# ConvFFN up and gate products as 2x2 blocks with seven products, on one Trainium2 core

## The chip, the cores and the metric

The kernel runs on one core of a Trainium2 chip. The metric is the device time of one execution in microseconds (us), the median of several runs. The engines of a core are named as the profile names them: PE is TensorE's matmuls and PEld its weight loads, DVE the vector engine, ACT the scalar engine, POOL GpSimd, SP the engine that issues the DMAs. Each of them works through its own queue in order.

## What is computed

A two-layer trunk: each layer is a mixer (layer 0 an mLSTM and a retention mixer, layer 1 an HGRN2 mixer) and then a ConvFFN. 592 tokens pass together (16 meta tokens, 8 samples of 8, a prompt of 512), the model width is 1024 and the ConvFFN's 2816. The change touches the ConvFFN:

```python
def rms_norm(x, gain):
    y = x * lax.rsqrt(jnp.mean(x * x, axis=-1, keepdims=True) + EPS)
    return y * gain

def conv_ffn(xn, w_in, conv_w, conv_b, w_out, buf):
    u, gate = jnp.split(xn @ w_in, 2, axis=-1)
    padded = jnp.concatenate([buf, u], axis=1)
    conv = conv_b + sum(padded[:, j:j + t] * conv_w[j] for j in range(3))
    h = jax.nn.silu(conv) * gate
    return h @ w_out, padded[:, t:]
```

The result is added to the residual x. All inputs and outputs are float32.

## The kernel before

Features lie on partitions, tokens on columns. A float32 product is made of three matmuls of a 22-bit type (fp32r): every operand is split into a high part (an ACT copy) and a low part (a DVE subtraction), and high x high, high x low and low x high are added in PSUM. The residual's split parts are the moving operand; a weight tile of 128 x 128 is the stationary one.

The dense work is a list of blocks. Each block is a pair of a loader, which issues the weights' DMA and their split, and a body, which issues the products and what follows them. `stream` (L280) takes the blocks in order and keeps two weight tiles loaded ahead; `weights` (L296) loads into one of two raw buffers (L303), splits on ACT (L308) and on DVE (L310) into one of three pairs of buffers. The split is issued where the block is fetched, that is, before the body of the block in front. `interleave` (L133) mixes the mixers' own instructions between the blocks; once issued, each engine keeps the order.

`dense` (L316) makes 128 output features of all tokens: for each of eight 128-row chunks k three matmuls on each of two halves of the tokens, all through L123: 48 matmuls, of 296 columns in layer 0 and of 290 and 288 in layer 1. A `hooks` entry runs something after chunk k's matmuls are issued. PSUM has two double tiles ("mm") for such products and four single ones ("px").

`ffn` (L463) makes the ConvFFN of a layer. Its 22 `in_block`s (L474) take one 128-feature chunk each: the up product (48 matmuls), then `up` (L507 to L527), which multiplies it by 1/rms of each token (`rb`, from `norm_rows` and `norm_bcast`, hooked into block 0) on DVE and sets the convolution's edges with small POOL copies (L517 to L526); then the gate product (48 matmuls), its multiplication by 1/rms (L491), the convolution as one ACT operation (L493) and two DVE ones (L495), SiLU on ACT (L497), the gating (L501, L502), and the split of the result (L505 on ACT, L506 on DVE) into one of eight slots. 7, 7 and 8 chunks make a group. `out_proj` (L410) multiplies a group with the output weights, one block for each of eight output chunks (the first two side by side), and adds to the residual on DVE (L424); in the last group it also makes the next norm's square sums (L223, L230) and the next split parts of the residual (L215, L216). In layer 1 the last group goes over the tokens in two spans of 320 and 256 columns ("dq" in the profile, single "px" tiles). `token_proj` (L349) makes token-major products with two half weights; layer 0 begins with two of these blocks.

Of the kernel before, what the change touches and what calls it, by code (L numbers as in the profile page):

```python
# [9 lines left out]
F32 = mybir.dt.float32  # L10
# [30 lines left out]
def shape_constants():  # L41
# [44 lines left out]
    # which of a 32-row block's keys the queries of the second halves take, level by level; and the diagonal  # L86
# [13 lines left out]
def trunk_kernel(ctx: ExitStack, tc: tile.TileContext, I, O):  # L100
# [32 lines left out]
    def interleave(dense, streams, active):  # L133
        """runs `streams` in order, up to `active` at once, and `dense` whenever all of them wait"""
# [26 lines left out]
    # ------------------------------------------------------------ helpers  # L161
# [29 lines left out]
    # ------------------------------------------------------------ constants and inputs  # L191
# [40 lines left out]
    def quick_root(y, x, n):  # L232
        """1 / sqrt(x): fewer steps, with a table that the scalar engine has to load"""
# [5 lines left out]
    def norm_rows(ts=range(5), root=rsqrt):  # L239
        """1 / rms, token-major"""  # L240
# [16 lines left out]
    def norm_bcast(groups=((0, 1, 2), (3, 4))):  # L257
        """1 / rms of each token on all partitions"""
# [18 lines left out]
    # ------------------------------------------------------------ dense products  # L277
    # A block is (load, body): load() emits the weights' DMA and their split, body(w) is a generator.
    def stream(blocks):
# [11 lines left out]
        while ahead:  # L291
            w, body = ahead.pop(0)
            fetch()
            yield from body(w)

    def weights(*views):  # L296
        """views: DRAM [128, k, n]; hi/lo f32r tiles of the same shape"""
        out = []
        for v in views:
            k = v[0].shape[1]  # L300
            n = sum(a.shape[2] for a in v)
            raw = wp.tile([128, k, n], F32, name="wr", tag="wr", bufs=2)
            o = 0  # L303
            for a in v:
                ld.dma_start(out=raw[:, :, o:o + a.shape[2]], in_=a)
                o += a.shape[2]
            hi = wp.tile([128, k, n], F32R, name="wh", tag="wh", bufs=3)
            S.copy(hi, raw)  # L308
            lo = wp.tile([128, k, n], F32R, name="wl", tag="wl", bufs=3)
            V.tensor_tensor(out=lo, in0=raw, in1=hi.bitcast(F32), op=ALU.subtract)  # L310
            out.append((hi, lo))
        return out
# [30 lines left out]
    def proj(w, c0, post, first=0, hooks=None):  # L343
        """feature-major projection of the tokens from `first`"""
        def body(ww):
            (p,), off = yield from dense(ww, acts_x(), first, hooks)
# [3 lines left out]
    def token_proj(w, pieces, emit, first=False, hook=None):  # L350
        """token-major projection onto the columns of `pieces`"""
# [12 lines left out]
        def body(halves):  # L364
            p = None
            if first:
                # as the chunks of the residual come in; the norm is ready when the products are
# [30 lines left out]
    def split(src, j, scale=None):  # L398
        """src (f32 [128, NT]) * scale -> slot pair j as hi/lo."""
# [10 lines left out]
    def out_proj(w, row0, acts, c0, gain, last, ready=None, spans=(None,)):  # L410
        """blocks that add acts() @ w[row0:] to the residual chunk by chunk.  The first chunks go side by side, so
        that the last of acts() has time to come."""
        def block(ocs, span):
# [4 lines left out]
            def body(ww):  # L418
# [3 lines left out]
                ps, off = yield from dense(ww, acts(), c0, span=span)  # L422
# [11 lines left out]
    def mix_proj(w, mixed, c0, gain, src):  # L434
        """the residual comes back, and the heads' outputs go into it, half of them at a time"""
# [25 lines left out]
    # ------------------------------------------------------------ ConvFFN  # L461
    def ffn(l, next_gain, spans=(None,)):
# [10 lines left out]

        def in_block(fc):  # L474
            def body(ww):
# [4 lines left out]
                cvo, stv = env["cvo"], env["st"]  # L480
                (pu,), off = yield from dense(ww[0:1], acts_x(), c0, hooks[0])
                if fc > 0:
                    ub, b0 = up(pu, off)
                (pg,), off = yield from dense(ww[1:2], acts_x(), c0, hooks[1])
                if fc == 0:
                    ub, b0 = up(pu, off)
                rb = state["rb"]
# [964 lines left out]
```

## Time and profile before

| | us |
|---|---|
| median of 3 runs | 1631.42 |
| lowest and highest run | 1631.22 and 1632.81 |
| span of the profiled execution | 1633.1 |
| TensorE busy in it | 1584.1 |
| DVE busy in it | 938.8 |
| ACT busy in it | 625.8 |
| POOL busy in it | 204.2 |

The profiler gives no time outside its span, so the profiled execution's own time is the 1633.1 us. Layer 0's ConvFFN begins near 378 us and layer 1's near 1196 us; the last products end near 1619 us. Busy times of TensorE are modelled from the starts of its instructions, so what a matmul costs is read from the distance of one start to the next.

### The profile page before, as it was taken

The numbers are of one execution on the slowest core, as the hardware profiler recorded it, in microseconds if no ns is written. First come the engines' busy times: TensorE is split into PE (matmuls) and PEld (weight loads), VectorE is DVE, ScalarE is ACT, GpSimd is POOL, SyncE is SP. The second block draws the span as 40 slices with busy tenths as digits, with TensorE's granted clock in tenths as the row PEclk, the third lists the DMA queues.
The fourth block names the chain that finished last, engine by engine and source line by source line (L and its number), as shares of the span: only waits on it lengthen the run. The fifth ranks groups of instructions, "written<-read, shape, count | busy, mean of one in ns | idle before, by whom it ended". The sixth has DMA issues, their size and how long they took to land. (4 is left out here: it accounts for less than half of the span.)

```text
span 1633.1 us, 32234 instructions
## 1 busy us (share of the span) xinstructions
PE 1584.1 (97%) x13508; PEld 1538.7 (94%) x13508; DVE 938.8 (57%) x1933; ACT 625.8 (38%) x1114; POOL 204.2 (13%) x402
## 2 busy tenths in 40 slices
PE   4999999999999999999999899999999999999997
PEld 4999999999999999999999798898999999999997
DVE  5576564757553454355546876766675535534565
ACT  3543434334331232233345466564443213322343
POOL 4000000000110110010002525333001101100102
PEclk9999999999999999999999999999999999999998
DMA  4334435433323222322422132223233232223244
GB/s 144 97 94 100 94 89 83 141 95 95 88 73 87 78 81 75 91 78 85 146 74 66 56 102 91 61 95 96 92 101 89 71 93 84 74 85 88 80 120 135
DMA packets 236049, 149.61 MB, mean 92 GB/s; under 512 B 7512, under 2 KB 227416, under 8 KB 235904
## 3 DMA queue, kind: packets, MB, share of 16 engines
q1 hardware_dynamic: 235904, 147.56, 31.9%
q8 instruction: 106, 1.74, 0.4%
q14 instruction: 39, 0.32, 0.1%
HBM read 132.89 MB, written 14.65 MB: 90 GB/s over the span
## 5 line engine op out<-in xcount | busy, mean ns | idle before, releaser
L123 PE MATMUL dp<-h,wh 128*128 128x296 f32 (+2 forms) x2176 | 477.8, 301 | 0.8 <-ACT v_c L661 0.5
L308 ACT CAST wh<-wr 128x1024 fp32r<-128x1024 f32 (+3 forms) x240 | 234.1, 978 | 625.2 <-PE dp L123 485.5
L123 PE MATMUL dp<-xl,wh 128*128 128x296 f32 (+2 forms) x2176 | 472.1, 298 | 0.0
L123 PE MATMUL dp<-h,wl 128*128 128x296 f32 (+2 forms) x2176 | 471.7, 298 | 0.0
L123 PEld LDWEIGHTS dp<-h,wh 128*128 128x128 f32 x2176 | 351.2, 189 | 4.3 <-issue 1.8
L123 PEld LDWEIGHTS dp<-h,wl 128*128 128x128 f32 x2176 | 352.1, 189 | 0.0
L123 PEld LDWEIGHTS dp<-xl,wh 128*128 128x128 f32 x2176 | 351.8, 189 | 0.0
L310 DVE TENSOR_TENSOR wl<-wr,wh 128x1024 fp32r<-128x1024 f32 (+3 forms) x240 | 273.8, 1141 | 76.3 <-ACT wh L308 73.0
L123 PE MATMUL dp<-bh,wh 128*128 128x296 f32 (+2 forms) x832 | 182.8, 300 | 2.0 <-DVE x L424 0.5
L123 PE MATMUL dp<-bh,wl 128*128 128x296 f32 (+2 forms) x832 | 179.7, 297 | 0.0
L123 PE MATMUL dp<-bl,wh 128*128 128x296 f32 (+2 forms) x832 | 179.5, 297 | 0.0
L424 DVE TENSOR_TENSOR x<-x,dp 128x592 f32<-128x592 f32 (+2 forms) x72 | 54.9, 763 | 153.1 <-PE dp L123 153.0
L123 PEld LDWEIGHTS dp<-bh,wh 128*128 128x128 f32 x832 | 134.0, 188 | 5.9 <-ACT wh L308 2.4
L491 DVE TENSOR_TENSOR gt<-dp,rb 128x592 f32<-128x592 f32 (+1 forms) x44 | 33.7, 767 | 179.9 <-PE dp L123 179.8
L123 PEld LDWEIGHTS dp<-bl,wh 128*128 128x128 f32 x832 | 134.4, 188 | 0.0
L123 PEld LDWEIGHTS dp<-bh,wl 128*128 128x128 f32 x832 | 134.2, 188 | 0.0
L123 PE MATMUL tp<-wh,h 128*128 128x256 f32 (+3 forms) x280 | 84.6, 303 | 19.0 <-ACT wh L308 11.8
L123 PE MATMUL tp<-wl,h 128*128 128x256 f32 (+3 forms) x280 | 81.2, 290 | 0.3 <-DVE wl L310 0.3
L123 PE MATMUL tp<-wh,xl 128*128 128x256 f32 (+3 forms) x280 | 79.7, 289 | 1.9 <-DVE xl L216 1.9
L495 DVE SCALAR_TENSOR_TENSOR cv<-ub,vec,cv 128x612 f32<-128x612 f32 (+1 forms) x88 | 74.1, 842 | 1.6
L123 PEld LDWEIGHTS tp<-wh,h 128*128 128x128 f32 (+1 forms) x280 | 52.3, 187 | 24.0 <-ACT wh L308 11.8
L497 ACT ACTIVATE cv<-cv 128x612 f32<-128x612 f32 (+1 forms) x44 | 31.1, 708 | 90.8 <-DVE cv L495 90.8
(425 smaller groups left out, 1933.8 us busy)
## 6 DMA issues: line engine op xcount, KB each, us to landing
wr<-in_w_ffn_in SPq DMA_DIRECT2D x88, 512.0 KB, 3.8
wr<-in_w_in_ab SPq DMA_DIRECT2D x32, 512.0 KB, 7.0
wr<-in_w_in_c SPq DMA_DIRECT2D x32, 512.0 KB, 4.1
wr<-in_w_ffn_out SPq DMA_DIRECT2D x32, 448.0 KB, 3.5
wr<-in_w_ffn_out SPq DMA_DIRECT2D x24, 512.0 KB, 3.8
x<-in_x SPq DMA_DIRECT2D x16, 296.0 KB, 5.1
out_H<-s_s SPq DMA_DIRECT2D x8, 576.0 KB, 2.9
wr<-in_w_out_ab SPq DMA_DIRECT2D x16, 256.0 KB, 2.9
```

The source lines that it names most:

```text
L123: T.matmul(out, lhsT=lhsT, rhs=rhs, **kw)
L308: S.copy(hi, raw)
L310: V.tensor_tensor(out=lo, in0=raw, in1=hi.bitcast(F32), op=ALU.subtract)
L424: V.tensor_tensor(out=x[oc][:, a:b], in0=x[oc][:, a:b], in1=p[:, off + a:off + b], op=ALU.add)
L491: V.tensor_tensor(out=gt[:, h0:], in0=pg[:, off + h0:off + NT], in1=rb[:, h0:], op=ALU.mult)
L495: V.scalar_tensor_tensor(out=cv[:, b0:612], in0=ub[:, b0 + j:612 + j], scalar=cw[j], in1=cv[:, b0:612], op0=ALU.mult, op1=ALU.add)
L497: S.activation(cv[:, b0:612], cv[:, b0:612], AF.Silu)
```

## The change

In each layer the first four chunks (`NOLD`) are made as before, the other 18 in `strassen_block`. It takes the up and the gate weights of a chunk as the two rows of a 2x2 block matrix (its columns are the halves of the model width) and the normed residual as the other (halves of the width by halves of the tokens), and makes the product with seven block products of 4 x 3 matmuls, with sums and differences before and after. Its four weight splits, w0 to w3, are the up weights as they are, two sums (sum12), the gate weights with a sum in one half (sum3), and a half-size sum (sum4), made on DVE (`quadrants`); the products are, in order, B11 and B21 with w0, T1 and T2 with w1, T4 with w2, B22 with w3, T3 with w2. The differences of the residual are made once a layer: blocks 1 and 2 norm and gain it (`norm_chunk`, ACT and POOL), split the parts that are used alone (`split_alone`, ACT and DVE), subtract (`differences`, POOL), and block 3 splits the differences (`split_differences`).

The weights' splits no longer stand where the block is fetched. A `Split` joins one line; at most three are made and not yet given back, and the next of the line is made when one is given back (`done`) or is asked for. The old blocks give their splits back when the body is issued, the new ones after each last use. The steps from convolution to split (`activate`) are put off: a new block or output block issues them one at a time (`step_later`), an old block all at its end. The output products come in groups of 4 chunks, one block (`out_pair`, two output chunks from one 4 x 256 weight tile) after each new block; the last six chunks stay in `out_proj`. The raw output weights have a buffer of their own (`alt`). `load_state`'s tile gets another shape, for a shared buffer. `proj`, `token_proj` and `out_proj` ask for their splits with `got`. Comments are taken out.

```diff
+    class Split:
+        def __init__(self, k, n, src, sums=None):
+            self.k, self.n, self.src, self.sums, self.made = k, n, src, sums, None
+            line.append(self)
...
+        def make(self):
+            self.sum_up()
+            src = self.src() if callable(self.src) else self.src
+            hi = wp.tile([128, self.k, self.n], F32R, name="wh", tag="wh", bufs=3)
+            S.copy(hi, src)
+            if line:
+                line[0].sum_up()
+            lo = wp.tile([128, self.k, self.n], F32R, name="wl", tag="wl", bufs=3)
+            V.tensor_tensor(out=lo, in0=src, in1=hi.bitcast(F32), op=ALU.subtract)
+            self.made = (hi, lo)
+        def get(self):
+            while self.made is None:
+                live.append(line.pop(0))
+                live[-1].make()
+            return self.made
+        def done(self):
+            live.remove(self)
+            pump()
+    def pump():
+        while line and len(live) < 3:
+            line[0].get()
...
             w, body = ahead.pop(0)
             fetch()
+            pump()
             yield from body(w)
+            for sp in w or ():
+                if sp in live:
+                    sp.done()
...
+    def quadrants(v1, v2):
+        r1, r2 = raw_weights([v1]), raw_weights([v2])
+        a11, a12, a21, a22 = r1[:, 0:4, :], r1[:, 4:8, :], r2[:, 0:4, :], r2[:, 4:8, :]
+        env = {}
+        def sum12():
+            env["s"] = s = tp.tile([128, 8, 128], F32, name="s12", tag="ve", bufs=2)
+            V.tensor_tensor(out=s[:, 4:8, :], in0=a21, in1=a22, op=ALU.add)
+            V.tensor_tensor(out=s[:, 0:4, :], in0=s[:, 4:8, :], in1=a11, op=ALU.add)
+        def sum3():
+            V.tensor_tensor(out=a21, in0=a21, in1=a11, op=ALU.add)
+        def sum4():
+            env["s4"] = s4 = tp.tile([128, 4, 128], F32, name="s4", tag="nums", bufs=2)
+            V.tensor_tensor(out=s4, in0=env["s"][:, 0:4, :], in1=a12, op=ALU.add)
+        return [Split(8, 128, r1), Split(8, 128, lambda: env["s"], sum12), Split(8, 128, r2, sum3),
+                Split(4, 128, lambda: env["s4"], sum4)]
...
+        def norm_chunk(c):
+            g = vec[:, V_NFFN + 8 * l + c:V_NFFN + 8 * l + c + 1]
+            xn[c] = ap.tile([128, NT], F32, name=f"xn{c}", tag=f"b{'hl'[c % 2]}{4 + c // 2}")
+            S.activation(xn[c], x[c], AF.Copy, scale=g)
+            G.tensor_tensor(out=xn[c], in0=xn[c], in1=state["rb"], op=ALU.mult)
...
+        def differences(c):
+            p, q = xn[c], xn[c + 4]
+            G.tensor_tensor(out=p[:, h1], in0=p[:, h1], in1=p[:, h2], op=ALU.subtract)
+            G.tensor_tensor(out=p[:, h2], in0=p[:, h2], in1=q[:, h2], op=ALU.subtract)
+            G.tensor_tensor(out=q[:, h2], in0=p[:, h1], in1=q[:, h2], op=ALU.add)
+            G.tensor_tensor(out=q[:, h1], in0=q[:, h2], in1=q[:, h1], op=ALU.subtract)
+        def split_differences():
+            for c in range(8):
...
+                S.copy(hi[:, 0:2 * n], xn[c][:, a0:NT])
+                V.tensor_tensor(out=lo[:, 0:2 * n], in0=xn[c][:, a0:NT], in1=hi[:, 0:2 * n].bitcast(F32),
+                                op=ALU.subtract)
...
+        def strassen_block(fc):
...
+                yield from product(a, w[0], 0, "B11", True)
+                S.copy(s1, a)
+                step_later()
+                b = px("sb")[:, 0:n]
+                yield from product(b, w[0], 4, "B21", True)
+                w[0].done()
...
+                up_edges(fc, ub)
+                step_later()
+                yield from product(c, w[1], 4, "T1", True)
+                step_later()
+                yield from product(a, w[1], 0, "T2", False)
+                S.copy(u2, a)
+                V.tensor_tensor(out=u2, in0=c, in1=u2, op=ALU.subtract)
+                w[1].done()
+                step_later()
+                d = px("sd")[:, 0:n]
+                yield from product(d, w[2], 4, "T4", True)
+                step_later()
+                yield from product(b, w[3], 0, "B22", True)
+                V.tensor_tensor(out=ub[:, 102 + m:614], in0=b, in1=u2, op=ALU.add)
+                up_state(fc, ub)
+                w[3].done()
+                step_later()
+                yield from product(a, w[2], 0, "T3", False)
+                S.copy(u3, a)
+                gt = tmp("gt")
+                V.tensor_tensor(out=gt[:, h2], in0=u3, in1=c, op=ALU.subtract)
+                V.tensor_tensor(out=gt[:, h1], in0=u3, in1=d, op=ALU.subtract)
+                activate(fc, ub, gt)
+                step_later()
+                w[2].done()
...
         def in_block(fc):
...
+                ww = got(ww)
+                if fc == 1:
+                    hooks = ({k: lambda k=k: norm_chunk(k // 2 + 4 * (k % 2)) for k in range(8)}, None)
+                elif fc == 2:
+                    hooks = ({k: lambda k=k: split_alone(k // 2 + 4 * (k % 2)) for k in range(8)},
+                             {4 + k: lambda k=k: differences(k) for k in range(4)})
...
+                if fc == NOLD - 1:
+                    split_differences()
...
+                activate(fc, ub, gt)
+                while later:
+                    step_later()
...
+        blocks = [block(fc) for fc in range(4)]
+        for a in range(0, 16, 4):
+            for j in range(4):
+                blocks += [block(a + 4 + j), out_pair(a, a + 4, j)]
+        blocks += [block(20), block(21)]
+        blocks += out_proj(w_out, 16 * 128, lambda: acts[16:22], h0, next_gain, True, all_made, spans)
```

## Rows read from the trace of the kernel before

**Rows 1.** The page's first part: the span, then busy us (share) xinstructions.
```profile
span 1633.1 us, 32234 instructions
PE 1584.1 (97%) x13508; PEld 1538.7 (94%) x13508; DVE 938.8 (57%) x1933; ACT 625.8 (38%) x1114; POOL 204.2 (13%) x402
```

**Rows 2.** The chain that ended last, layer 1's ConvFFN: start, us, what.
```profile
1207.99 89.50 PE dp L123 x672
...
1309.29 134.10 PE dp L123 x1008
```

**Rows 3.** A window, layer 0's block 1: us, busy us of engines, PEclk, DMA share, GB/s.
```profile
391.85:404.90 13.05, 13.05 (x96) 13.05 (x97) 7.03 (x10) 5.11 (x7) 2.04 (x7) 1.00 0.28 82
```

**Rows 4.** Timeline of PE, last output span of layer 1: start, us, engine, line.
```profile
1603.81 0.28 PE L123 MATMUL dq<-bh,wl 128*128 128x256 f32 x1
...
1608.39 0.28 PE L123 MATMUL dq<-bh,wl 128*128 128x256 f32 x1
```

**Rows 5.** Groups of DVE instructions by form: xcount | busy us, mean ns | idle before.
```profile
L310 DVE TENSOR_TENSOR wl<-wr,wh 128x1024 fp32r<-128x1024 f32 x172 | 211.3, 1229 | 62.0 <-ACT wh L308 58.9
...
L310 DVE TENSOR_TENSOR wl<-wr,wh 128x512 fp32r<-128x512 f32 x32 | 21.9, 685 | 2.6 <-ACT wh L308 2.5
...
L1153 DVE TENSOR_TENSOR e<-gate,e 128x296 f32<-128x296 f32 x16 | 7.4, 461 | 0.0
```

**Rows 6.** Timeline of all engines: one chunk's chain after its gate product, layer 0.
```profile
418.24 0.77 DVE L491 TENSOR_TENSOR gt<-dp,rb 128x592 f32<-128x592 f32 x1 [4.36 <-PE dp L123]
...
420.16 1.74 DVE L495 SCALAR_TENSOR_TENSOR cv<-ub,vec,cv 128x612 f32<-128x612 f32 x2
...
421.94 0.72 ACT L497 ACTIVATE cv<-cv 128x612 f32<-128x612 f32 x1 [2.15 <-DVE cv L495]
...
422.85 0.69 DVE L502 TENSOR_TENSOR gt<-gt,cv 128x512 f32<-128x512 f32 x1
...
423.57 0.69 ACT L505 CAST bh<-gt 128x592 fp32r<-128x592 f32 x1 [0.91 <-DVE gt L502]
...
424.43 1.05 ACT L308 CAST wh<-wr 128x1024 fp32r<-128x1024 f32 x1 [0.17 <-PE dp L123]
```

**Rows 7.** Timeline of DVE, layer 0's block 2: an evacuation and a remainder.
```profile
412.07 0.68 DVE L524 TENSOR_TENSOR ub<-dp,rb 128x512 f32<-128x512 f32 x1
412.67 1.22 DVE L310 TENSOR_TENSOR wl<-wr,wh 128x1024 fp32r<-128x1024 f32 x1
```

**Rows 8.** Timeline of POOL in the same microsecond.
```profile
412.33 0.19 POOL L520 COPY ub<-ub 128x2 f32<-128x2 f32 x1
...
412.81 1.12 POOL L525 COPY cvo<-ub 128x2 f32<-128x2 f32 x1
```

**Rows 9.** Timeline of POOL, the start and layer 1's mixer.
```profile
19.22 1.17 POOL L225 TENSOR_TENSOR ssq<-x 128x592 f32<-128x592 f32 x1 [17.50 <-DMA x<-in_x]
...
22.60 1.85 POOL L230 TENSOR_TENSOR ssq<-ssq,sq 128x592 f32<-128x592 f32 x1
...
892.15 1.77 POOL L1135 TENSOR_TENSOR ex<-bl 128x296 f32<-128x296 f32 x1
...
1015.79 0.68 POOL L1137 TENSOR_TENSOR ex<-bl 128x296 f32<-128x296 f32 x1
```

**Rows 10.** Timeline of PE at the start, after a pause.
```profile
38.45 0.23 PE L123 MATMUL ssp<-mean,ssq 128*80 128x1 f32 x1 [3.19 <-DVE ssq L1343]
```

**Rows 11.** A window after that pause.
```profile
40.00:43.00 3.00, 3.00 (x16) 3.00 (x15) 2.17 (x10) 1.06 (x1) 0.00 (x0) 0.50 0.23 54
```

**Rows 12.** The chain near the end: a weight load and the next cast.
```profile
1605.63 4.37 DMA wr<-in_w_ffn_out
...
1610.09 1.06 ACT wh L308
```

**Rows 13.** The groups by form again: the remainder of a 1040-column weight half.
```profile
L310 DVE TENSOR_TENSOR wl<-wr,wh 128x1040 fp32r<-128x1040 f32 x4 | 5.7, 1428 | 11.7 <-ACT wh L308 11.7
```

More of the change, by code (lines that the diff above doesn't have):

```diff
@@ L293, in stream @@
             fetch()
+            pump()
             yield from body(w)
-    def weights(*views):
[L298 to L312, printed above, removed]
+            for sp in w or ():
+                if sp in live:
+                    sp.done()
@@ new lines, in raw_weights @@
+    def raw_weights(v, alt=False):
+        k = v[0].shape[1]
+        n = sum(a.shape[2] for a in v)
+        if alt:
+            raw = ap.tile([128, 1776], F32, name="wr1", tag="u1")[:, 0:k * n].rearrange("p (k n) -> p k n", k=k)
+        else:
+            raw = wp.tile([128, k, n], F32, name="wr", tag="wr", bufs=2)
+        o = 0
+        for a in v:
+            ld.dma_start(out=raw[:, :, o:o + a.shape[2]], in_=a)
+            o += a.shape[2]
+        return raw
+    def weights(*views):
+        return [Split(r.shape[1], r.shape[2], r) for r in map(raw_weights, views)]
@@ L345, in body @@
         def body(ww):
-            (p,), off = yield from dense(ww, acts_x(), first, hooks)
+            (p,), off = yield from dense(got(ww), acts_x(), first, hooks)
             post(p[:, off + first:off + NT])
@@ L421, in body @@
                 a, b = span or (c0, NT)
-                ps, off = yield from dense(ww, acts(), c0, span=span)
+                ps, off = yield from dense(got(ww), acts(), c0, span=span)
                 for oc, p in zip(ocs, ps):
@@ new lines, in ffn, with step_later, activate, tap @@
+        later = []
+        def step_later():
+            if later:
+                later.pop(0)()
+        def activate(fc, ub, gt):
+            cw = [vec[:, V_CW + l * 66 + j * 22 + fc:V_CW + l * 66 + j * 22 + fc + 1] for j in range(3)]
+            cb = vec[:, V_CB + l * 22 + fc:V_CB + l * 22 + fc + 1]
+            env_ = {}
+            def tap():
+                cv = env_["cv"] = tmp("cv", 612)
+                S.activation(cv[:, b0:612], ub[:, b0:612], AF.Identity, scale=cw[0], bias=cb)
+            def taps():
+                cv = env_["cv"]
+                for j in (1, 2):
+                    V.scalar_tensor_tensor(out=cv[:, b0:612], in0=ub[:, b0 + j:612 + j], scalar=cw[j],
+                                           in1=cv[:, b0:612], op0=ALU.mult, op1=ALU.add)
+            def silu():
+                S.activation(env_["cv"][:, b0:612], env_["cv"][:, b0:612], AF.Silu)
+            def gating():
+                cv = env_["cv"]
+                cvs = cv[:, 0:100].rearrange("p (s i) -> p s i", i=10)[:, s0:, 0:8]
+                gts = gt[:, h0:80].rearrange("p (s i) -> p s i", i=8)
+                V.tensor_tensor(out=gts, in0=gts, in1=cvs, op=ALU.mult)
+                V.tensor_tensor(out=gt[:, P0:], in0=gt[:, P0:], in1=cv[:, 100:612], op=ALU.mult)
+            def high():
+                env_["hi"] = slot("bh", fc % 8, F32R)
+                S.copy(env_["hi"][:, h0:], gt[:, h0:])
+            def low():
+                hi, lo = env_["hi"], slot("bl", fc % 8, F32R)
+                V.tensor_tensor(out=lo[:, h0:], in0=gt[:, h0:], in1=hi[:, h0:].bitcast(F32), op=ALU.subtract)
+                acts[fc] = (hi, lo)
+            later.extend((tap, taps, silu, gating, high, low))
@@ new lines, in out_pair, with body @@
+        def out_pair(a, b, j):
+            def body(w):
+                while any(acts[fc] is None for fc in range(a, b)):
+                    step_later()
+                hi, lo = w[0].get()
+                for i in range(2):
+                    (p,), off = yield from dense([(hi[:, :, 128 * i:128 * i + 128], lo[:, :, 128 * i:128 * i + 128])],
+                                                 acts[a:b], h0)
+                    if i:
+                        w[0].done()
+                    oc = 2 * j + i
+                    V.tensor_tensor(out=x[oc][:, h0:], in0=x[oc][:, h0:], in1=p[:, off + h0:off + NT], op=ALU.add)
+                    step_later()
+            v = w_out[a * 128:b * 128, :].rearrange("(k p) n -> p k n", p=128)[:, :, 256 * j:256 * j + 256]
+            r = lambda: raw_weights([v], True)
+            return (lambda: [Split(4, 256, r())], body)
@@ L529, in in_block, with all_made @@
+                V.tensor_tensor(out=gt[:, h0:], in0=pg[:, off + h0:off + NT], in1=state["rb"][:, h0:], op=ALU.mult)
+                activate(fc, ub, gt)
+                while later:
+                    step_later()
             return (lambda: weights([cols(w_in, fc * 128)], [cols(w_in, DFF + fc * 128)]), body)
+        def all_made():
+            while later:
+                step_later()
+            return True
         acts = [None] * NFC
-        blocks = [in_block(fc) for fc in range(8)]
@@ L534, in ffn @@
-        out = lambda a, b, *more: out_proj(w_out, a * 128, lambda: acts[a:b], h0, *more)
-        blocks += out(0, 7, None, False) + [in_block(fc) for fc in range(8, 15)]
-        blocks += out(7, 14, None, False) + [in_block(fc) for fc in range(15, 22)]
-        blocks += out(14, 22, next_gain, True, None, spans)
+        block = lambda fc: in_block(fc) if fc < NOLD else strassen_block(fc)
+        blocks = [block(fc) for fc in range(4)]
+        for a in range(0, 16, 4):
+            for j in range(4):
+                blocks += [block(a + 4 + j), out_pair(a, a + 4, j)]
```

134 lines of the change are left out of this document (90 added, 44 removed).

## The prediction

> **What bounds the kernel now.** I read the page's busy shares first [rows 1]: TensorE is busy 1584.1 of 1633.1 us, the vector engine (DVE) 938.8; the scalar engine (ACT) and GpSimd (POOL) less. Then the chain that ended last in the second ConvFFN [rows 2]: unbroken stretches of hundreds of matmuls (two of them are shown), with little between. Then a window inside a ConvFFN [rows 3]: TensorE fills it wholly, at a granted clock of 1.00. So a ConvFFN costs its count of matmuls times the time from one to the next. Ninety-six products of a chunk pair took 13.05 us in layer 0, 136.0 ns each; in layer 1, 672 took 89.50 us, 133.2 ns each.
>
> The profiled execution spans 1633.1 us, 1.7 above the median of 1631.42. I work out a difference on the trace and take it off the median. A measurement of this kernel can tell about 0.2%, 3.3 us, from no change.
>
> **Fewer products (removed).** Pairs 4 to 21 of each layer, 18 of 22, have 7 x 4 x 3 = 84 matmuls for 96. Layer 0 keeps 296 columns: 12 x 136.0 ns = 1.63 us a pair, 29.4 us. Layer 1 goes from 290 and 288 columns to 290, about 0.4 ns a matmul: 12.79 - 84 x 133.6 ns = 1.57 us a pair, 28.2 us. Together 57.6 us. Each weight tile now serves one matmul instead of two in a row. The products of the last output half, where a weight serves one matmul, start 117 ns apart at 256 columns (the first and last of 40 stand in [rows 4]); the 40 fewer columns and 19 ns less leave no surcharge for it, so I take none. The Trainium skill (TensorE: Matmul & The Clock Gate, "Back-to-back issue gap") gives columns over 2.4 GHz plus 2.5 ns for an isolated matmul: 125.8 ns in place of the 136.0 here, and an estimated saving of 53.1 us in place of 57.6; the same section has a stream with weight loads paced by both, and the rows, which show more, decide. The output products stay 1056 a layer; groups of 4 only move them.
>
> **A period in the steady state (added on DVE, ACT).** One seven-product block and one output block of two chunks take 84 + 48 matmuls: 17.95 us in layer 0, 17.6 in layer 1. Durations on DVE: 1024 columns 1.23 us, 512 0.69, 296 0.46 [rows 5], 592 0.77, two taps 1.74 [rows 6]. Five 512 sums or parts (sum12 is two) and the 512 remainder come to 3.4, three 1024 remainders 3.7, six evacuations and sums of halves 2.5, taps 1.7, gating 0.9, low part 0.8; the output block adds 1.2 and 1.5. That is 15.7 us; queued operations start 0.08 earlier than durations say (0.60 apart for 0.68 long [rows 7]), so about 14 of 17.95. ACT has 3.4 + 1.1 casts and some 3 us more. Neither exceeds TensorE. Being in order matters more. From the block's start, in the order issued: T1's weights must be ready at 3.3 and are made one block before; w3 is cast when B21 ends at 3.3, done 4.6, due 8.2; the output weights are made at 7.0 to 9.2, due 11.4; the next w0 at 9.9 to 12.7, due 17.95; the next w2 at 18.0 to 20.2, due 24.5. The closest is PSUM: the second output chunk, at 14.7, needs the pair's accumulator, which DVE frees at 13.1 to 13.5, behind two sums and a remainder. That leaves 1.2 us. So I cost the steady state at nothing.
>
> **Getting into it (moved and added, on the path).** The weights' line holds three splits at once, and a block of two weights gives its slots back only after its activation steps are issued. So the gate weight of blocks 1 to 3, formerly split while the up product ran, now stands behind the previous block's whole chain: gate multiply, two taps, silu, gating, high part, cast, remainder. Its links show the length [rows 6]: 0.8 + 1.7 + 0.75 + 0.9 + 0.7 + 1.0 + 1.2 = 7.2 us from the previous gate's end, while the remainder is due at 6.53 + 0.54 = 7.07. By itself that costs 0.2. But POOL gets new work ahead of the edge copies that the first tap needs: eight 592-column multiplies in block 1, sixteen 296-column differences in block 2.
>
> The port price: a 2-column POOL copy takes 0.19 us beside a DVE operation that reads PSUM and 1.12 while a DVE remainder with two SBUF inputs runs, ending with it [rows 7, 8]. So I add the two engines' SBUF work, one operation each in turn. POOL alone took 1.17 for 592 columns and 0.68 for 296, in turn 1.85 and 1.77 [rows 9]; I take 1.12 and 0.64 queued, plus the DVE operations between. The Trainium skill says the same of this port (SBUF — State Buffer, "SBUF: two separate sides"): an exclusive lock for the whole instruction. It speaks against this change; by free overlap, the other reading, the entry below would cost about 16 us instead of 22, with this lock it costs the 22.
>
> Layer 0, in us from block 1's up product (391.85 in the trace):
> - Block 1's gate weight is ready at 7.25, 0.2 late. The split of block 2's first weight holds DVE to 8.4. POOL multiplies 8.4 + 8 x 1.12 = 17.4, edge copies to 17.9, then tap to remainder 7.3: block 2's gate weight is whole at 25.3, due 20.3, 4.95 late.
> - TensorE stood over 4 us there. In the trace a pause of 3.19 us before 38.45 [rows 10] is followed by a granted clock of 0.50, 1.2 of 2.4 GHz, from 40 to 43: 16 matmuls in 3 us [rows 11], where 117 ns each [rows 4] would make 25. That lost 9 x 117 ns and more with the edges; at 296 columns I take 1.6 us. Gate 2 ends at 32.85.
> - POOL's differences start at 32.1, behind the block's edge copies, and alternate with taps, gating, low part and remainder. Block 3's gate weight is whole at 43.05, due 39.9: 3.15 late. Gate 3 ends at 49.05.
> - Block 4's second raw half takes the buffer of that weight, so its load goes out at 43.05. From such a remainder's end to the next cast 4.4 us passed [rows 12]: 47.45. The sum for T1's and T2's weights waits for it at the head of DVE: sum12 to 48.9, w0's remainder 50.1, block 3's up 50.95; only then is the accumulator free (due 49.05).
> - Eight remainders of the differences, 0.70 each: 56.55. Then block 3's chain, 0.7 + 1.7 + 0.75 + 0.85 + 0.7, T1's weight cast 1.05 and sum3 and remainder: 63.9. T1's product ends at 65.3, and 66.9 with the clock, as TensorE stood 8 us. Without waits it would end at 3 x 13.06 + 4.9 = 44.1.
> Loss 22.8 us in layer 0, 22 in layer 1 (fewer edges, shorter products): 44.8.
>
> **Smaller terms.** The second token-major product of layer 0: its second half weight comes behind the emits; cast 1.05 and remainder 1.43 [rows 13] against 1.4 us of first products: 1.3, bounds 0 and 2.5. End of layer 1: the first output pair of the last group reaches chunk 21 after 30 matmuls, 4.5 us, while its chain takes 7.8: 3.3; bounds 0 and 5. In layer 0 it has 60 matmuls, 8.2 us, no cost. The first split of the line elsewhere stands where it stood; 0. Loads: 1.5 MB a period, as dense as before, 0.28 of the DMA engines [rows 3]; 0. Comments and the state tile's shape: 0.
>
> **Sum.** -57.6 + 44.8 + 1.3 + 3.3 = -8.2: 1623.2 us. Bounds for one entry: 16 (no port turns, POOL at 0.68 and 1.12, no clock loss) to 33 (POOL at 1.85 and 1.2 to 1.77 throughout, +6 and +4 to 5). So -57.6 + 32 + 0 = -25.6 to -57.6 + 66 + 7.5 = +16.
>
> **The rivals.**
> 1. A cheap entry: port turns mostly hidden, the load early. 2 x 16, with half the small terms: -57.6 + 32 + 2.3 = -23.3, 1608. For: POOL runs 0.68 undisturbed when DVE waits. Against: the waits on the load and on T1's weight need no POOL.
> 2. A dear entry: POOL at its contended rows. 2 x 31 + 4.6: +9, 1640, slower. It decides once an entry passes 26.5 us. For: the 1.77 and 1.85 rows. Against: in block 1 DVE has little to do.
> 3. The steady state slips: DVE frees the accumulator too late for the second output chunk. It decides when the run of half sum, sum12, remainder and evacuation takes over 1.2 us longer than added up. At 1.7 us, 0.5 a period and 32 periods give 16: 1639, slower. For: five in-order operations behind a cast. Against: about 3.5 us of DVE's period is free.
> 4. The products shrink and the entry hides behind work that I took as serial: at most 5 an entry, 1631.4 - 57.6 + 10 + 3 = 1587. Against: every link above is an in-order queue.
>
> **How the numbers follow.** Forecast (entry 19 to 27 us) 0.50, 1616 to 1632; cheap entry 0.20; dear entry 0.14; slipping steady state 0.12; hidden entry 0.04. Faster by over 0.2% (below 1628.2): 0.38 of the forecast's 0.50, all of the cheap and hidden: 0.62. Within: 0.11 + 0.04 + 0.03 = 0.18. Slower: 0.01 + 0.10 + 0.09 = 0.20. The range from 1604 to 1641 takes in the cheap and most of the dear and slipping cases; outside stay the hidden case and the far ends of 2 and 3, under 2 in 10.
>
> **What would show it.** Right: 84 and 48 matmuls without a gap in the periods, 11.4 + 6.5 us; TensorE waiting in the gate products of blocks 2 and 3 on their weights' casts and remainders, and longest at T1 of block 4, on a cast or remainder of its second weight; a granted clock of 0.50 after it; POOL's eight multiplies ending about 17 us after block 1 starts. Wrong: a gap on x or the accumulator in each period (rival 3); an entry under 17 or over 28 us (1, 2); a DVE wait at sum12 without a load before it; matmuls with single-use weights over 137 ns apart, 3024 of them, 3 us for each ns.

## The result, and the profile after

The changed kernel takes 1609.15 us in the median (1607.46 to 1614.75) beside 1632.12 for the kernel before: a ratio of 0.9861, 95% interval [0.9843, 0.9879], about 23 us faster. A second time beside other runs it took 1612.86, ratio 0.9873 [0.9856, 0.9889]. The forecast was 8.2 us faster, 1623.2; the first rival, the cheap entry, had 1608. The profiled execution, from which the rows come, took 1614.75 us and has a span of 1612.6, 20.5 less than that of before.

The page of the changed kernel: the span, the busy times (compare [rows 1]), and the group of matmuls in which TensorE (PE) waited most for DVE (busy us, mean ns, then the idle time ahead and what ended it).

```profile
span 1612.6 us, 32125 instructions
PE 1536.5 (95%) x13076; PEld 1488.0 (92%) x13076; DVE 1166.3 (72%) x2321; ACT 743.7 (46%) x1342; POOL 251.6 (16%) x450
...
L123 PE MATMUL dp<-h,wh 128*128 128x296 f32 (+2 forms) x1024 | 231.4, 308 | 14.4 <-DVE ub L568 13.8
```

432 matmuls fewer, as the diff says; DVE has 227 us more. Where TensorE stood at the two entries is seen in its own rows, layer 0 first, then layer 1 (start, duration, and in brackets the idle time ahead and what ended it):

```profile
412.23 0.83 PE L123 MATMUL dp<-h,wh 128*128 128x296 f32 x2 [4.41 <-DVE ub L568]
...
431.62 0.83 PE L123 MATMUL dp<-h,wh 128*128 128x296 f32 x2 [4.70 <-DVE ub L568]
...
451.72 0.41 PE L123 MATMUL ac<-h,wh 128*128 128x296 f32 x1 [1.62 <-ACT cs L687]
...
1215.72 0.82 PE L123 MATMUL dp<-h,wh 128*128 128x290 f32 x2 [4.49 <-DVE ub L568]
...
1249.99 0.41 PE L123 MATMUL ac<-h,wh 128*128 128x290 f32 x1 [2.97 <-ACT cs L687]
```

The first two are the up products of blocks 2 and 3, waiting for the accumulator of the up product before, which DVE evacuates at L568, and the fourth is block 2's again; the third and fifth are T1 of the first seven-product block, waiting for an ACT copy (L687), not for T1's weight. Windows of the same kernel (busy us and instructions of each engine, the granted clock, DMA) show the clock after these pauses, and a steady period of layer 1 as the last row, comparable with [rows 3]:

```profile
404.00:408.00 4.00, 3.82 (x29) 3.57 (x27) 4.00 (x4) 2.59 (x3) 4.00 (x3) 1.00 0.00 0
408.00:412.00 4.00, 0.00 (x0) 0.00 (x0) 4.00 (x6) 2.02 (x5) 3.92 (x5) 0.99 0.00 0
412.00:416.00 4.00, 3.77 (x17) 3.81 (x18) 4.00 (x5) 1.58 (x3) 3.84 (x4) 0.59 0.40 116
428.00:432.00 4.00, 0.38 (x1) 0.41 (x2) 3.25 (x6) 2.77 (x4) 1.58 (x7) 0.62 0.00 0
432.00:436.00 4.00, 4.00 (x18) 4.00 (x18) 0.60 (x1) 0.61 (x1) 0.83 (x3) 0.53 0.44 131
1294.22:1311.82 17.60, 17.60 (x135) 17.60 (x134) 14.23 (x24) 7.87 (x12) 0.62 (x3) 1.00 0.31 95
```

After a pause the clock is near 0.5 to 0.6, as in [rows 11]; 18 matmuls start in 4 us where 29 would. The steady period is full: 17.60 us with TensorE busy for all of it, as forecast, and DVE for 14.23, near the forecast's 14.

To weigh the entries I take, in each layer, the time from the norm's first product (`ssp`) to the second product of block 5, and subtract what the kernel without the entry work (second experiment) took without a wait: 67.6 us in layer 0, 66.5 in layer 1. The changed kernel loses 16.3 and 10.8 us, 27.1 together; the forecast had 22.8 and 22, and named an entry under 17 as a sign that it is wrong.

### The profile page after: what moved, and what is told of

It is laid out like the page before. It is cut to its first block, busy times and chain, and to the rows that moved or that the text cites. A ratio compares the mean times of both kernels' runs of the same rounds, so it can differ in the third digit from the quotient of the medians.

```text
span 1612.6 us, 32125 instructions
## 1 busy us (share of the span) xinstructions
PE 1536.5 (95%) x13076; PEld 1488.0 (92%) x13076; DVE 1166.3 (72%) x2321; ACT 743.7 (46%) x1342; POOL 251.6 (16%) x450
## 5 line engine op out<-in xcount | busy, mean ns | idle before, releaser
L295 ACT CAST wh<-wr 128x1024 fp32r<-128x1024 f32 (+3 forms) x240 | 232.5, 970 | 383.9 <-PE dp L123 104.5
L123 PE MATMUL dp<-h,wh 128*128 128x296 f32 (+2 forms) x1024 | 231.4, 308 | 14.4 <-DVE ub L568 13.8
L123 PE MATMUL dp<-xl,wh 128*128 128x296 f32 (+2 forms) x1024 | 225.0, 301 | 0.0
L123 PE MATMUL dp<-h,wl 128*128 128x296 f32 (+2 forms) x1024 | 224.8, 300 | 0.0
L123 PEld LDWEIGHTS dp<-h,wh 128*128 128x128 f32 x1024 | 166.8, 192 | 18.5 <-ACT bh L606 9.3
L123 PEld LDWEIGHTS dp<-xl,wh 128*128 128x128 f32 x1024 | 168.2, 191 | 0.0
L123 PEld LDWEIGHTS dp<-h,wl 128*128 128x128 f32 x1024 | 168.0, 191 | 0.0
L123 PE MATMUL ac<-h,wh 128*128 128x296 f32 (+1 forms) x432 | 129.9, 301 | 7.7 <-ACT cs L687 4.6
L123 PE MATMUL ac<-h,wl 128*128 128x296 f32 (+1 forms) x432 | 128.6, 298 | 0.0
L123 PE MATMUL ac<-xl,wh 128*128 128x296 f32 (+1 forms) x432 | 128.1, 297 | 0.0
L295 ACT CAST wh<-s 128x1024 fp32r<-128x1024 f32 x72 | 60.2, 836 | 57.2 <-PE sb L123 35.0
L123 PE MATMUL sb<-b2h,wh 128*128 128x296 f32 (+1 forms) x288 | 85.9, 298 | 0.2 <-DVE ub L700 0.2
```

The lines of the kernel that those rows point to most:

```text
L123: T.matmul(out, lhsT=lhsT, rhs=rhs, **kw)
L295: S.copy(hi, src)
```

## The experiments

All are the changed kernel but for the edit named. The loss is the measure just given.

| kernel | median, us | ratio to before, interval | loss, layer 0 + layer 1 |
|---|---|---|---|
| changed | 1609.15 | 0.9861 [0.9843, 0.9879] | 16.3 + 10.8 |
| changed, again | 1612.86 | 0.9873 [0.9856, 0.9889] | 16.8 + 10.4 |
| old products | 1636.87 | 1.0022 [1.0007, 1.0038] | no seven-product block |
| no entry work | 1584.05 | 0.9695 [0.9675, 0.9716] | 0 + 0.8 |
| no multiply | 1609.34 | 0.9849 [0.9830, 0.9868] | 14.6 + 11.3 |
| second half early | 1607.57 | 0.9835 [0.9814, 0.9855] | 13.2 + 8.5 |
| short multiply | 1600.00 | 0.9792 [0.9777, 0.9807] | 9.4 + 5.3 |
| short POOL | 1586.82 | 0.9709 [0.9695, 0.9724] | 1.3 + 0.8 |
| multiply on DVE | 1596.31 | 0.9764 [0.9737, 0.9791] | 6.3 + 4.5 |
| all on DVE | 1594.73 | 0.9757 [0.9730, 0.9783] | 2.6 + 4.8 |
| source order | 1628.96 | 0.9963 [0.9949, 0.9976] | 24.0 + 17.7 |
| DVE and early half | 1592.53 | 0.9747 [0.9728, 0.9766] | 2.5 + 4.4 |
| third raw buffer | 1592.77 | 0.9749 [0.9726, 0.9773] | 2.5 + 3.0 |

**Old products.** Everything but the seven-product blocks.

```diff
-        NOLD = 4
+        NOLD = NFC
...
```

> The changed kernel with no seven-product block: all 22 pairs of each layer are made as before, and the norm, split and differences of the residual are not made; the line of splits, the put-off steps and the output groups of 4 stay. Theory A (the products save their full 57.6 us; what the profile of the changed kernel shows as waits and lower clock at the two entries, 15.9 + 10.6 us, and 2.3 us of waits on DVE's L707 late in layer 0, belong to the seven-product blocks; the 6.5 us lost in the last output group belongs to the groups of 4): 1609.2 + 57.6 - 28.8 = 1638, 6 above the kernel before. Rival B (the line of splits itself makes the entries wait, with or without the new work): 1609.2 + 57.6 = 1667, or at least above 1650. Rival C (the loss in the last group comes from the seven-product blocks in front of it): 1632, as before.

Measured 1636.87, 0.22% above before: theory A's time, though only 2.2 us above the kernel before that ran beside it, where A has 6. Rival B is out: no matmul waits over 0.25 us at the two entries, so the line of splits makes nobody wait by itself. Rival C is out by the rows: the loss in the last output group is there without any seven-product block; its waits (engine, line, what it waited for: us in total, times, longest), from 1560 us on, are

```profile
PE dq L123 <- ACT wh L295: 2.1, 3, 1.2
...
PE dq L123 <- DVE wl L299: 1.2, 3, 0.5
```

**No entry work.**

```diff
-                    hooks = ({k: lambda k=k: norm_chunk(k // 2 + 4 * (k % 2)) for k in range(8)}, None)
...
-                    hooks = ({k: lambda k=k: split_alone(k // 2 + 4 * (k % 2)) for k in range(8)},
-                             {4 + k: lambda k=k: differences(k) for k in range(4)})
...
-                S.copy(hi[:, 0:2 * n], xn[c][:, a0:NT])
...
+                hi, lo = state[c]
...
```

> The seven-product blocks stay, but the residual is not normed, split or subtracted for them (no norm_chunk, split_alone, differences, split_differences): their operands are halves of the residual's split parts that are there already, so the up and gate products are other numbers. Theory A (the entries' 26.5 us come from that work on POOL and DVE): 1609.2 - 26.5 = 1583 if all goes; the wait of the first sum (L368) for its load, 3.7 us in layer 0 and 4.7 in layer 1, and T1's second weight behind it can leave up to 5: 1583 to 1588. Rival B (the weights' line: block 2's and 3's weights wait for the slots of the block in front, and the load does the rest): the entries stay at 16 or more together: 1599 to 1609.

Measured 1584.05: theory A, and the load at the first sum leaves TensorE no wait when DVE is free. Against the kernel with the old products it is 52.8 us faster. Its rows still have 3.1 us of waits on the half sum that is L707 in the changed kernel (below), so by this difference the fewer products are worth about 56 of the 57.6 forecast.

**No multiply.**

```diff
             S.activation(xn[c], x[c], AF.Copy, scale=g)
-            G.tensor_tensor(out=xn[c], in0=xn[c], in1=state["rb"], op=ALU.mult)
```

> POOL's eight multiplications by 1/rms a layer (L626) are left out, so the residual of the seven-product blocks is not normed; splits and differences stay. Theory A1 (POOL's multiplications, at 1.83 us in the median beside DVE, hold DVE's remainders of L637 and L646 and behind them the up product's evacuation L568): the wait before block 2's up product goes (4.4 us in each layer, with 1.4 of lower clock in layer 0), and the differences, earlier by about 12 us, are done before block 3 needs DVE (4.7 us of wait and 2.1 of clock in layer 0, 1 to 2 in layer 1): 1609.2 - 10 = 1599 to 1609.2 - 18 = 1591. Rival A2 (DVE's own added work, eight remainders and eight more, is the cause, POOL only a bystander): the DVE operations stand where they stood: 1606 to 1609. Rival B (weights' line): 1609.

Measured 1609.34: A1's time is wrong, and so is A2's reason. The waits before blocks 2 and 3 are gone from the rows, but new ones stand in block 0, at the broadcast of 1/rms (TensorE's rows):

```profile
395.20 0.65 PE L123 MATMUL rbp<-dg,ones 128*128 128x336 f32 x1 [6.03 <-DVE dg L269]
...
400.39 0.58 PE L123 MATMUL rbp<-dg,ones 128*128 128x256 f32 x1 [2.00 <-DVE dg L270]
```

Without the dependence on 1/rms the splits and POOL's differences run before it, between the small DVE steps that make it. So this edit moved the collision instead of taking it away, and could not tell the theories apart. The kernels below keep the dependence.

**Second half early.**

```diff
...
-        r1, r2 = raw_weights([v1]), raw_weights([v2])
+        r1, r2 = raw_weights([v1]), raw_weights([v2], alt)
...
-            return (lambda: quadrants(cols(w_in, fc * 128), cols(w_in, DFF + fc * 128)), body)
+            return (lambda: quadrants(cols(w_in, fc * 128), cols(w_in, DFF + fc * 128), fc == NOLD), body)
...
-            r = lambda: raw_weights([v], True)
+            r = lambda: raw_weights([v], a + j > 0)
```

> The second raw weight half of each layer's first seven-product block is loaded into the output weights' own buffer, which is idle until then, and the first output weight into the shared one, so that this load no longer waits for block 3's gate weight. Nothing else is changed. Theory L (the load at the head of DVE's queue sets the first T1): DVE's wait before the first sum, 3.7 and 4.7 us, goes, and with it T1's waits, 1.6 + 0.8 us in layer 0 and 3.0 in layer 1: 1609.2 - 5.4 = 1604. Rival D (DVE's work sets it; it would only wait elsewhere): 1608 to 1609. Rival E (the first output weight now comes late, as its buffer is freed only by block 3's gate weight): up to 3 us a layer more, 1612 to 1615.

The first T1 no longer waits in either layer, and the loss falls by 5.5 us (27.1 to 21.7), as theory L has it. Of this the medians show 1.6, the ratios 4, and the two intervals overlap, so the reading rests on the rows.

**Short multiply, and short POOL.**

```diff
-            G.tensor_tensor(out=xn[c], in0=xn[c], in1=state["rb"], op=ALU.mult)
+            G.tensor_tensor(out=xn[c][:, 0:64], in0=xn[c][:, 0:64], in1=state["rb"][:, 0:64], op=ALU.mult)
```

> POOL's eight multiplications a layer (L626) go over 64 of 592 columns (the other columns of the seven-product blocks' residual are not normed), still behind 1/rms, so nothing can run ahead of it as it did without them; all DVE and ACT work stays as it was. Theory P (POOL's SBUF operations stretch DVE's, one at a time, and DVE then frees the up product late): about 8 x 1.1 to 1.8 us of POOL's time less in block 1, DVE's remainders there back to 0.45 and 0.77 us, the wait before block 2's up product (4.4 us in each layer, 1.4 of lower clock in layer 0) goes; block 3's (4.7 and 2.1 in layer 0) shrinks as the differences come earlier: 1609 - 10 = 1599, to 1592 if block 3's wait goes too. Theory Q (DVE's own added operations set the waits): 1606 to 1609.

Measured 1600.00, at the upper end of theory P. In the second kernel the four differences also go over 32 columns each (`p[:, h1]` becomes `p[:, a0:a0 + 32]`, and so on).

> As the one before, and POOL's sixteen differences a layer go over 32 of 296 columns too, so POOL has next to no work at the entries, while DVE and ACT keep all of theirs (eight and eight remainders, the casts); the residual's normed parts and differences are not made on the other columns. Theory P: all waits before block 2's and 3's up products go, 13.3 and 6.9 us from the norm to block 4's first product; T1's wait on the load stays, 3.1 and 4.2: 1609 - 20 = 1589. Theory Q: most waits stay: 1604 or more.

Measured 1586.82, with 2.1 us of loss left of 27.1, though DVE and ACT did all of their work. T1's wait, which was expected to stay, went as well. The durations say why DVE was done earlier. The two kinds of remainder that blocks 1 and 2 make on DVE, from 386 to 462 us (busy us, mean ns), in the changed kernel,

```profile
L646 DVE TENSOR_TENSOR b2l<-xn,b2h 128x592 fp32r<-128x592 f32 x4 | 6.2, 1561 | 0.0
L637 DVE SCALAR_TENSOR_TENSOR b11l<-xn,b11h 128x296 fp32r<-128x296 f32 x4 | 6.2, 1559 | 0.0
```

and in the kernel with short POOL operations:

```profile
L646 DVE TENSOR_TENSOR b2l<-xn,b2h 128x592 fp32r<-128x592 f32 x4 | 3.3, 824 | 0.0
L637 DVE SCALAR_TENSOR_TENSOR b11l<-xn,b11h 128x296 fp32r<-128x296 f32 x4 | 2.1, 532 | 0.6 <-ACT b11h L636 0.6
```

**Multiply on DVE, and all on DVE.**

```diff
-            S.activation(xn[c], x[c], AF.Copy, scale=g)
-            G.tensor_tensor(out=xn[c], in0=xn[c], in1=state["rb"], op=ALU.mult)
+            V.scalar_tensor_tensor(out=xn[c], in0=x[c], scalar=g, in1=state["rb"], op0=ALU.mult, op1=ALU.mult)
```

> The gain (ACT) and the multiplication by 1/rms (POOL) are one DVE operation for each of the eight chunks, and the rest is as it was. Theory P (what counts is the sum of DVE's and POOL's time on SBUF, taken in turn): DVE gets 8 x 0.77 = 6.2 us, POOL loses 8 x 1.1 to 1.8, so 3 to 8 us a layer less in front of block 2's evacuation, of which the waits of 4.4 a layer and 1.4 of clock can go: 1599 to 1606. Theory Q (DVE's queue alone counts): 6.2 us a layer more, 1615 to 1621.

> As the one before, and the sixteen differences a layer are on DVE as well (0.46 us each, 7.4 us), so POOL has no work at the entries but the edge copies. Theory P: 10 to 20 us of POOL's turns a layer less against 13.6 of DVE's more: 1600 to 1609, and no DVE operation longer than in the steady state. Theory Q: DVE's queue gets 13.6 us a layer longer: 1625 to 1636.

In the second the differences' `G.tensor_tensor` become `V.tensor_tensor` (the lines move up by one). Measured 1596.31 and 1594.73: theory P in both, a little better than its bounds. (ACT is spared the eight gains here too; short POOL, where ACT kept them, shows that this isn't needed.) The whole program's DVE was already the busier engine, it got 13.6 us a layer more, and the kernel became 14 us faster. Each of its operations took its own time again (from 386 to 462 us, all on DVE):

```profile
L645 DVE TENSOR_TENSOR b2l<-xn,b2h 128x592 fp32r<-128x592 f32 x4 | 3.1, 767 | 0.0
L636 DVE SCALAR_TENSOR_TENSOR b11l<-xn,b11h 128x296 fp32r<-128x296 f32 x4 | 1.8, 458 | 0.0
```

**Source order.** `tie` is given for the first seven-product block alone.

```diff
+        def second():
+            if tie is not None:
+                tie(env["s"])
+            return env["s"]
...
+                for lo in (ops["T2", 3][1], acts[NOLD - 1][1][:, P0:NT]):
+                    V.scalar_tensor_tensor(out=s[:, 4, 0:1], in0=lo[:, 0:1].bitcast(F32), scalar=0.0,
+                                           in1=s[:, 4, 0:1], op0=ALU.mult, op1=ALU.add)
```

> The changed kernel, with the second split (T1's and T2's weight) of each layer's first seven-product block tied behind block 3's chain and behind the eighth remainder of the differences, by two one-column DVE operations that add zero times their results: the order in which the source has them, and which the prediction's walk took for granted. Theory O (the walk was wrong because DVE made this weight ahead of the eight remainders and of block 3's chain): T1 is ready 64 us after block 1's start instead of 57, the losses go back to the walk's 22.8 and 22 from 16.4 and 11.2: 1609 + 6 + 11 = 1626, at least 1618. Rival (the order of these made no difference, since something else held T1): 1607 to 1612.

Measured 1628.96: theory O. T1 of each layer, in TensorE's rows:

```profile
457.52 0.62 PE L123 MATMUL ac<-h,wh 128*128 128x296 f32 x1 [7.55 <-ACT wh L295]
...
1262.84 0.61 PE L123 MATMUL ac<-h,wh 128*128 128x290 f32 x1 [8.40 <-ACT wh L295]
```

Block 1 starts at 394.5 there (block 2's first row at 411.95, less its wait of 4.42 and 96 x 136.0 ns), so T1 comes 63.0 us after it; the forecast's walk has the weight whole at 63.9. T1 now waits for its weight (`wh`, L295), as the walk had it, and not for L687. The loss, 41.8 us, is within 3 of the forecast's 44.8; 24.0 of it is in layer 0, where 22.8 was forecast, and 17.7 in layer 1, where the forecast had 22 without a walk of its own.

**DVE and early half, and a third raw buffer.** The first joins two edits shown above. The second adds

```diff
...
-            return (lambda: weights(*views), body)
+            return (lambda: weights(*views, alt=third and ocs[0] in (2, 5)), body)
```

> Multiplication and differences on DVE, as in the kernel with all of it on DVE (1594.7), and the second raw half of the first seven-product block loaded early, as before. Theory L: the waits that are left at the first T4 (1.6 + 0.3 us and the lower clock behind it, 3.2 us in layer 0, 5 in layer 1) hang on sums behind the load; with the load early they go: 1587. Rival D (they hang on DVE's queue, full of eight remainders at that time): 1592 to 1596.

> As the one before, and in the last output groups of both layers two of eight weights go through the output weights' own raw buffer, so that three loads can be on the way instead of two. Theory G (the last group's 5.5 us in layer 1, where the products of 6 chunks take 2.1 to 2.5 us a weight, are waits for loads that are issued too late): 2 to 4 us less than the kernel before it, about 1584. Rival (DVE and ACT splits or the sums behind set it): no difference over 1 us.

The early half is a miss: 2.2 us, not the 7.7 of theory L and less than the spread of the runs, and T4 still waits, 1.04 and 1.66 us, as rival D says. The sum that its weight needs (L372) stands behind all eight remainders on DVE. The third buffer takes the last group from 45.4 to 43.4 us in the trace, the least that theory G has; the medians, 1592.53 and 1592.77, don't show it. These kernels, with the two that precede the source order, are faster than both the kernel before and the changed one: 1592.53 is 0.9747 [0.9728, 0.9766] of before.

**Changed again.**

> The changed kernel once more, beside the others. Theory N (the 3.2 us wait at 278 us in the mixer of its first profile, behind a load, is a chance of that execution): the wait is gone and the profiled execution is near the median, 1607 to 1610, with the same waits at the two entries (27.6 us together, within 2). Rival (the wait belongs to the changed order of loads): it is there again.

The median is 1612.86, above the 1610 of theory N. The loss is the same, 27.1, and so is the wait in the mixer, 3.22 us: the rival. More on it below.

## Why the prediction was right and wrong

| term | forecast | in the trace |
|---|---|---|
| fewer products | -57.6 | about -56 by old products against no entry work |
| steady state | 0 | +2.3, three waits on L707 late in layer 0 |
| two entries | +44.8 | +27.1 |
| second token-major product | +1.3 | 0 (8.4 us in both kernels) |
| end of layer 1 | +3.3 | about +5.5 |
| all else up to layer 0's ConvFFN | 0 | about +2, -0.7 in the second profile |

These come to -19; the spans differ by -20.5.

**The step that failed is the order of the walk into the steady state**, and with it the wait that the walk put in front of T1. So the term of the two entries, 44.8, was 17.7 too large. The walk took each engine's work in the order of the source: "Eight remainders of the differences, 0.70 each: 56.55. Then block 3's chain" and only then T1's weight, 63.9. The rows of DVE and ACT in the changed kernel have another order:

```profile
398.37 1.73 DVE L637 SCALAR_TENSOR_TENSOR b11l<-xn,b11h 128x296 fp32r<-128x296 f32 x1
...
401.99 2.04 DVE L646 TENSOR_TENSOR b2l<-xn,b2h 128x592 fp32r<-128x592 f32 x1
...
411.40 0.67 DVE L568 TENSOR_TENSOR ub<-dp,rb 128x512 f32<-128x512 f32 x1
...
445.31 1.22 DVE L299 TENSOR_TENSOR wl<-s,wh 128x1024 fp32r<-128x1024 f32 x1
446.44 4.88 DVE L663 TENSOR_TENSOR xl<-xn,h 128x592 fp32r<-128x592 f32 x7
...
452.61 0.85 DVE L591 SCALAR_TENSOR_TENSOR cv<-ub,vec,cv 128x612 f32<-128x612 f32 x1
...
444.84 4.21 ACT L662 CAST h<-xn 128x592 fp32r<-128x592 f32 x7
448.95 1.04 ACT L295 CAST wh<-wr 128x1024 fp32r<-128x1024 f32 x1
449.91 0.68 ACT L662 CAST h<-xn 128x592 fp32r<-128x592 f32 x1
450.49 0.89 ACT L586 ACTIVATE cv<-ub,vec 128x612 f32<-128x612 f32 x1
451.29 0.38 ACT L687 COPY cs<-ac 128x296 f32<-128x296 f32 x1
```

T1's weight (the remainder of `s`, 445.31) runs ahead of the eight remainders (L663) and of block 3's taps (452.61). It is whole at 446.5, 51.8 us after block 1's start (394.8), and T1 starts 57.0 us after it. What T1 waited for in between is ACT's copy of B11 (L687): the two products lie in one double tile, and the copy, whose input was there when B21 began (448.29), stood in ACT's queue behind the casts of the differences (L662), another weight's cast and block 3's first convolution step (L586). The walk has no such wait. Forcing the source's order brought the walk's number back, which shows that the order made the difference. Nor does each engine keep the order of the source, as the description of the kernel before may be read. The same reordering put `split_alone`, written in block 2's hooks, into block 1 (398.37), ahead of the evacuation of block 1's up product (411.40). So the first wait was not at block 2's gate weight, as forecast, but at block 2's up product, which needs that accumulator. That its length came out near, 4.41 us for 4.95, is luck, as it is another wait. The wait at block 3's up product, which only layer 0 has, comes from the order on POOL:

```profile
412.08 1.81 POOL L655 TENSOR_TENSOR xn<-xn,xn 128x296 f32<-128x296 f32 x1
...
422.67 0.83 POOL L656 TENSOR_TENSOR xn<-xn 128x296 f32<-128x296 f32 x1
423.44 0.19 POOL L547 COPY ub<-ub 128x2 f32<-128x2 f32 x1
...
423.78 0.90 ACT L586 ACTIVATE cv<-ub,vec 128x612 f32<-128x612 f32 x1 [10.20 <-POOL ub L548]
424.72 2.19 DVE L591 SCALAR_TENSOR_TENSOR cv<-ub,vec,cv 128x612 f32<-128x612 f32 x2 [6.05 <-ACT cv L586]
```

Twelve of the sixteen differences, which began at 409.3 (14.5 us after the block's start, not 32.1), stood ahead of the edge copies of block 1's up product, which DVE had finished at 412.1. The convolution and DVE's taps waited for these copies, DVE idle for 6.05 us, and the next evacuation, behind the taps, came late. That POOL's new work holds up the edge copies is what the forecast said; which differences stood ahead of which copies it had wrong. The trace of before could have warned: its DVE has a weight's remainder between two steps of 1/rms, which `norm_rows` issues in one go:

```profile
1200.96 0.17 DVE L187 TENSOR_TENSOR rs_a<-rt 128x5 f32<-128x5 f32 x1
1201.04 1.23 DVE L310 TENSOR_TENSOR wl<-wr,wh 128x1024 fp32r<-128x1024 f32 x1
1202.18 0.16 DVE L188 SCALAR_TENSOR_TENSOR rs_a<-rs_a,ms 128x5 f32<-128x5 f32 x1
```

**The port turns were real, their price was not right.** POOL's eight multiplications, in turn with DVE:

```profile
393.70 2.89 POOL L626 TENSOR_TENSOR xn<-xn,rb 128x592 f32<-128x592 f32 x2
...
397.69 11.25 POOL L626 TENSOR_TENSOR xn<-xn,rb 128x592 f32<-128x592 f32 x6
```

They end at 408.9, 14.2 us after the block's start, where 17.4 was forecast: they took 1.80 us each in place of the 1.12 taken, but began before the block and not 8.4 us into it, so two errors partly cancel. All but 2.1 us of the loss went when POOL's operations were cut short, and most when DVE did them. Both edits take away the port turns and POOL's queue ahead of the edge copies together; how much of the loss belongs to each is not shown. The Trainium skill (SBUF — State Buffer, "SBUF: two separate sides") has an exclusive lock for a whole instruction on the pair of ports that GpSimd and a DVE operation with two SBUF inputs share. The trace agrees: 1561 and 1559 ns for remainders that take 767 and 458 alone, while an evacuation, which reads PSUM, still took 0.67 us (411.40) beside a difference on POOL.

**The products** were right, to 2 of 57.6 us by the difference of two kernels. By the rows they were closer: the 132 matmuls of a steady period in layer 1 take 17.60 us, 133.3 ns each, where 133.2 was read before. **The steady state** was right but for three places. Its weak point is the first sum at the head of DVE's queue, which waits there for its load, 49.2 us in 34 waits over the run; late in layer 0 the load came later, and the half sum that frees T3's accumulator stood behind it:

```profile
712.37 0.40 PE L123 MATMUL ac<-h,wh 128*128 128x296 f32 x1 [1.14 <-DVE cs L707]
```

This is the third rival's mechanism, with a load in front in place of long sums, at a seventh of its price (2.3 us for 16). **The end of layer 1** cost 5.5 us, just over the bound of 5, and not for the reason given: chunk 21's chain cost 0.2 us. The last group takes 45.3 us for 288 matmuls, where before 53.0 for 384 would make 39.8. The weights of 6-chunk products last 2.1 to 2.5 us on TensorE, and two raw buffers seem not to bring them as fast: the third buffer took 2.0 us back. The rest of the 5.5 stays open.

**The rivals.** The cheap entry had the right time, and not its reason: T1's weight cost nothing and the load 5.5 of 27.1 us (second half early), but the port turns were not hidden, as DVE's remainders of 1.56 us show. That its 1608 is so near the measured 1609 is luck in part: the entries cost 27.1 for its 32, the smaller terms near 10 for its 2.3.

## What to carry to other kernels

Before walking through a transient by hand, look in the trace for the order that the engines were really given: where two rows stand the other way round than in the source, a walk in the source's order has no ground. Where two engines share a port, add up both engines' time on it; work moved to the busier one can end sooner. An edit that takes away work can also take away the dependence that held other work in its place, so shorten an operation rather than remove it when its cost is the question.

## What was not expected of the hardware

Loads of equal size landed sooner or later in different programs. ACT's second cast of the first weights came at 15.07 us in the changed kernel and 18.41 before, as its load landed earlier, which made the first norm 3.3 us earlier. Near 275 us it is the other way: a cast of the mixer's weights waits for its load in the changed kernel, and TensorE behind it:

```profile
273.14 1.05 ACT L295 CAST wh<-wr 128x1024 fp32r<-128x1024 f32 x1 [6.04 <-DMA wr<-in_w_in_ab]
...
277.87 0.31 PE L127 MATMUL p<-csm,bl 128*80 128x128 f32 x1 [3.24 <-DVE bl L1119]
```

In the kernel before the wait of that matmul is 0.44 us, with the old products 0.24, and in all eleven profiles of kernels with seven-product blocks that follow the change it is 2.5 to 6.3. From 260 to 280 us the DMA engines are busy for 0.83 of the time and move 86 GB/s, where before it was 0.73 and 94. Why was not tried and stays open. The two nearly cancel: layer 0's ConvFFN norm begins at 385.3 us in the changed kernel's first profile, at 382.2 in its second, and at 383.0 in the kernel before.
